# Two overlapping load slots in place of three separate ones, in a max-pooling kernel that streams its input

## The chip, the cores and the metric

The kernel runs on one core of a Trainium2 chip. The metric is the device time of one execution in microseconds (us).

A **window** here is one pooling window: 16 floats, 64 B, of which the maximum is kept. A load of n windows moves n x 64 B into each of the 128 partitions, that is n x 8192 B in all.

DVE is the vector engine, which does the poolings; SP and ACT are the engines that issue DMAs here. A DMA is spread over the core's 16 DMA engines: by the packet records each of them moves 8 of its 128 rows, one packet per row, and then signals a completion semaphore, a counter on which other engines wait. Where the text says that engines end apart, these 16 are meant.

## The reference, cut to what matters

```python
def setup_inputs():
    batch, channels, length = 32, 256, 4096
    output_size = 256
    return {"x": np.random.randn(batch, channels, length).astype(np.float32), ...}

def reference(x, output_size):
    for i in range(output_size):
        start = int(i * length / output_size)          # windows of 16
        end = int((i + 1) * length / output_size)
        result[:, :, i] = np.max(x[:, :, start:end], axis=-1)
    return result
```

134.22 MB are read, 8.39 MB are written, and nothing is read twice. Each partition handles 16384 windows.

## The kernel before

All the on-chip memory that the kernel uses is one area. At its low end are three load slots; from its high end the results grow downwards. As the results grow, the slots must shrink, so loads go from 1024 windows to 736.

```python
    SLOTS = 3
    MOST = 65536 // (4 * W)           # 1024 windows: 64 KB per partition
    FIRST = 128
    ...                               # sizes: 128, 1024 x2, 1000 x3, 940 x3, 884 x3,
    ...                               #        832 x3, 784 x3, 736, 152
    for g, loads in enumerate(groups):
        ...
        for i, size in enumerate(loads):
            a = b - size
            at = n_loads % SLOTS * slot_sizes[n_loads // SLOTS] * W
            slot = area[:, at : at + size * W]
            nc.sync.dma_start(out=slot, in_=xg[:, a * W : b * W])
            nc.vector.reduce_max(
                out=area[:, base + a : base + b],
                in_=slot.rearrange("p (n w) -> p n w", w=W),
                axis=mybir.AxisListType.X,
            )
            n_loads += 1
            b = a
        ...
    for dst, src in stores[1:2] + stores[0:1] + stores[2:]:
        nc.sync.dma_start(out=dst, in_=src)
```

Loads and stores are all issued from one engine (SP) into one queue. A load into a slot waits until the pooling of what was there is done. With three slots, two more loads are in the queue meanwhile.

## Time and profile before

| | kernel before |
|---|---|
| device time | 335.2 us (3 runs, 335.18 to 335.23) |
| span of the profiled run | 333.4 us |
| DMA queue busy | 99.2% of the span |
| DVE busy | 276.0 us (83%) |
| DMAs | 20 loads and 4 stores |

Lines of the page of the kernel before: busy time by engine, DMA packets, the DMA queue (packets, MB, share of the 16 DMA engines' time), the issues of the 1000-window loads (size, median us from issue to landing):

```profile
DVE 276.0 (83%) x20; POOL 0.2 (0%) x4
...
DMA packets 3456, 142.61 MB, mean 428 GB/s; under 512 B 384, under 2 KB 512, under 8 KB 512
...
q1 hardware_dynamic: 3456, 142.61, 99.2%
...
area<-in_x_dram SPq DMA_DIRECT2D x3, 8000.0 KB, 39.9
```

The queue is never idle between 1.75 and 332.1 us. A load takes 39.9 us from issue to landing, though it flows for only 19, because it stands in line behind another one.

The timeline of the kernel before. Columns: start in us, duration, engine, line, operation, result and input shapes, and in brackets the idle time before it and what ended that:

```profile
5.60 2.29 DVE L82 TENSOR_REDUCE area<-area 128x128 f32<-128x2048 f32 x1 [5.60 <-DMA area<-in_x_dram]
24.95 17.22 DVE L82 TENSOR_REDUCE area<-area 128x1024 f32<-128x16384 f32 x1 [17.06 <-DMA area<-in_x_dram]
44.30 17.22 DVE L82 TENSOR_REDUCE area<-area 128x1024 f32<-128x16384 f32 x1 [2.13 <-DMA area<-in_x_dram]
63.20 16.82 DVE L82 TENSOR_REDUCE area<-area 128x1000 f32<-128x16000 f32 x1 [1.68 <-DMA area<-in_x_dram]
...
281.35 13.22 DVE L82 TENSOR_REDUCE area<-area 128x784 f32<-128x12544 f32 x1 [1.54 <-DMA area<-in_x_dram]
296.18 13.22 DVE L82 TENSOR_REDUCE area<-area 128x784 f32<-128x12544 f32 x1 [1.61 <-DMA area<-in_x_dram]
```

DVE waits before every pooling but the last, so each of these starts when its load lands. The distance between two starts is the time in which one load flows: 19.35 us for 1024 windows, 14.83 for 784, in both cases 0.0189 us per window, whatever the size. The time is therefore the bytes over a fixed rate, plus a start, an end and small costs per DMA.

### The profile page before, as it was taken

What the parts mean: (1) busy time and instruction counts of PE and PEld (TensorE: products, weight loads), DVE (VectorE), ACT (ScalarE), POOL (GpSimd) and SP (SyncE); (2) the same over time, 40 slices, a digit from 0 to 9 for tenths busy, and PEclk for the clock granted to TensorE, in tenths of its full rate; (3) what the DMA queues carried; (4) which work ended last, traced back from release to release, by engine and by line L of the source; (5) the groups of instructions that cost most, each with busy time, mean ns of one, the idle gap of its engine ahead of it and who ended that gap; (6) DMA issues with size and microseconds to landing.
All of it is one profiled execution on the core that took longest, in us unless ns stands there. A gap on an engine that the chain in (4) does not pass through costs nothing.

```text
span 333.4 us, 113 instructions
## 1 busy us (share of the span) xinstructions
DVE 276.0 (83%) x20; POOL 0.2 (0%) x4
## 2 busy tenths in 40 slices
DVE  2009979797988989797989797989898898989990
POOL 0000000000000000000000000000000000000000
DMA  9898989898989998999999999999999999999997
GB/s 377 377 503 377 503 369 491 369 491 369 491 369 462 462 462 346 462 462 441 434 434 434 434 434 415 409 409 505 415 409 433 433 433 433 433 416 452 391 432 333
DMA packets 3456, 142.61 MB, mean 428 GB/s; under 512 B 384, under 2 KB 512, under 8 KB 512
## 3 DMA queue, kind: packets, MB, share of 16 engines
q1 hardware_dynamic: 3456, 142.61, 99.2%
HBM read 134.22 MB, written 8.39 MB: 428 GB/s over the span
## 4 chain that ended last, share of the span: by engine, by line
DMA 64%; DVE 31%; DVEq 1%; another core or an unknown queue 0%; SPq 0%; issue 0%
DMA area<-in_x_dram 64%; DVE area L82 31%; DVEq L129 1%; SPq L81 0%; DVEq L82 0%
## 5 line engine op out<-in xcount | busy, mean ns | idle before, releaser
L82 DVE TENSOR_REDUCE area<-area 128x1000 f32<-128x16000 f32 (+8 forms) x20 | 276.0, 13806 | 49.2 <-DMA area<-in_x_dram 49.2
L115 POOL MEMSET const-bfloat16-1.0<- 128x1 bf16 x1 | 0.1, 102 | 0.0
L115 POOL MEMSET const-uint8-127<- 128x1 uint8 x1 | 0.1, 102 | 0.0
L115 POOL MEMSET const-float32-0.0<- 128x1 f32 x1 | 0.1, 99 | 0.2 <-issue 0.2
L115 POOL MEMSET const-float32-1.0<- 128x1 f32 x1 | 0.1, 99 | 0.0
## 6 DMA issues: line engine op xcount, KB each, us to landing
area<-in_x_dram SPq DMA_DIRECT2D x3, 8000.0 KB, 39.9
area<-in_x_dram SPq DMA_DIRECT2D x3, 7520.0 KB, 37.5
area<-in_x_dram SPq DMA_DIRECT2D x3, 7072.0 KB, 35.3
area<-in_x_dram SPq DMA_DIRECT2D x3, 6656.0 KB, 33.2
area<-in_x_dram SPq DMA_DIRECT2D x3, 6272.0 KB, 31.3
area<-in_x_dram SPq DMA_DIRECT2D x1, 5888.0 KB, 30.3
out_dram<-area SPq DMA_DIRECT2D x1, 3934.0 KB, 27.4
out_dram<-area SPq DMA_DIRECT2D x1, 2966.0 KB, 33.7
```

Source lines behind the costliest of these rows:

```text
L82: nc.vector.reduce_max(out=area[:, base + a : base + b], in_=slot.rearrange("p (n w) -> p n w", w=W), axis=mybir.AxisListType.X,)
L115: nc = _bacc.Bacc("TRN2", target_bir_lowering=False, num_devices=1)
L129: with _tile.TileContext(nc) as tc:
```

## The change: intent and diff

The intent is fewer and larger transfers: 17 loads in place of 20. Two slots of 64 KB are left, and each swings by a gap of 152 windows (9.5 KB): a load lies alternately at the low and at the high end of its place. The part that the next load into the same place will cover (868 windows of 1020) is pooled first; the next load waits for that part only, and the other 152 windows are pooled afterwards. The results get memory of their own, so the loads no longer shrink.

```diff
-    SLOTS = 3
-    MOST = 65536 // (4 * W)
...
+    CHUNK = 1020
+    GAP = 152
+    FIRST = 152
+    LOADS_A, LOADS_B = 9, 6
...
+    ring = pool.tile([P, 2 * (CHUNK + GAP) * W], fp32, tag="ring", name="ring")
+    kept = pool.tile([P, total - last], fp32, tag="kept", name="kept")
...
+            low = n_loads % 2 * (CHUNK + GAP)
+            moved = n_loads // 2 % 2
+            at = low + moved * GAP
+            nc.sync.dma_start(
+                out=ring[:, at * W : (at + n) * W], in_=xg[:, a * W : (a + n) * W]
             )
+            if n == CHUNK:
+                dst = kept[:, base + a : base + a + n]
+                cut = CHUNK - GAP if moved else GAP
+                parts = [(0, cut), (cut, n)]
+                for u, v in parts if moved else parts[::-1]:
+                    pooled(dst[:, u:v], at + u, v - u)
+            else:
+                end = (at + CHUNK) * W
+                last_kept = ring[:, end - n : end]
+                pooled(last_kept, at, n)
...
+    for dst, src in stores:               # 9180, 152, 6120, 932 columns
         nc.sync.dma_start(out=dst, in_=src)
```

The changed kernel has loads of 152, 15 x 1020 and 932 windows and four stores.

More of the change, by code (lines that the diff above doesn't have):

```diff
@@ L32 @@
     assert B * C * O % P == 0
-    AREA = 53200
-    SLOTS = 3
-    MOST = 65536 // (4 * W)
-    ALIGN = 4
-    FIRST = 128
-    ROUNDS_A = 3
-    LAST = 4
-    slot_sizes = [MOST]
-    rounds = [[FIRST] + [MOST] * (SLOTS - 1)]
-    left = total - sum(rounds[0])
-    while left:
-        room = AREA - (total - left)
-        n = min(room // (SLOTS * W + SLOTS) // ALIGN * ALIGN, MOST)
-        if left <= slot_sizes[-1]:
-            n = left
-        slot_sizes.append(n)
-        rounds.append([])
-        while left and len(rounds[-1]) < SLOTS:
-            n = min(n, left)
-            rounds[-1].append(n)
-            left -= n
@@ L57 @@
-    sizes = [n for r in rounds for n in r]
-    groups = [sizes[:1], sizes[1 : ROUNDS_A * SLOTS], sizes[ROUNDS_A * SLOTS :]]
+    CHUNK = 1020
+    GAP = 152
+    FIRST = 152
+    LOADS_A, LOADS_B = 9, 6
+    last = total - FIRST - (LOADS_A + LOADS_B) * CHUNK
+    assert 0 < last and last * (W + 1) <= CHUNK * W
     pool = ctx.enter_context(tc.tile_pool(name="pool", bufs=1))
-    area = pool.tile([P, AREA], fp32, tag="area", name="area")
+    ring = pool.tile([P, 2 * (CHUNK + GAP) * W], fp32, tag="ring", name="ring")
@@ L63, with pooled, group @@
+    kept = pool.tile([P, total - last], fp32, tag="kept", name="kept")
     xw = x.flatten_outer_dims().rearrange("r (o w) -> (r o) w", w=W)
     ow = out.flatten_outer_dims().rearrange("r o -> (r o)")
+    def pooled(dst, at, n):
+        nc.vector.reduce_max(
+            out=dst,
+            in_=ring[:, at * W : (at + n) * W].rearrange("p (n w) -> p n w", w=W),
+            axis=mybir.AxisListType.X,
+        )
+    taken = 0
+    def group(n):
+        nonlocal taken
+        span = slice(taken * P, (taken + n) * P)
+        taken += n
+        return (
+            xw[span].rearrange("(p n) w -> p (n w)", p=P),
+            ow[span].rearrange("(p n) -> p n", p=P),
+        )
@@ L66 @@
+    xg, first_og = group(FIRST)
+    first_kept = kept[:, 0:FIRST]
+    nc.sync.dma_start(out=ring[:, CHUNK * W : (CHUNK + FIRST) * W], in_=xg)
+    pooled(first_kept, CHUNK, FIRST)
     stores = []
     n_loads = 0
-    first = 0
-    low = AREA
-    for g, loads in enumerate(groups):
-        n = sum(loads)
-        xg = xw[first : first + P * n].rearrange("(p n) w -> p (n w)", p=P)
-        og = ow[first : first + P * n].rearrange("(p n) -> p n", p=P)
-        first += P * n
-        base = low - n
-        b = n
-        for i, size in enumerate(loads):
-            a = b - size
-            at = n_loads % SLOTS * slot_sizes[n_loads // SLOTS] * W
-            slot = area[:, at : at + size * W]
-            nc.sync.dma_start(out=slot, in_=xg[:, a * W : b * W])
-            nc.vector.reduce_max(
-                out=area[:, base + a : base + b],
-                in_=slot.rearrange("p (n w) -> p n w", w=W),
-                axis=mybir.AxisListType.X,
-            )
-            n_loads += 1
-            b = a
-        low = base
-        if g < len(groups) - 1:
-            stores.append((og, area[:, base : base + n]))
-        else:
-            end = sum(loads[len(loads) - LAST :])
-            for a, b in ((end, n), (0, end)):
-                stores.append((og[:, a:b], area[:, base + a : base + b]))
@@ L97 @@
-    for dst, src in stores[1:2] + stores[0:1] + stores[2:]:
+    base = FIRST
+    for loads in ([CHUNK] * LOADS_A, [CHUNK] * LOADS_B + [last]):
+        xg, og = group(sum(loads))
+        a = 0
+        for n in loads:
+            low = n_loads % 2 * (CHUNK + GAP)
[3 more added lines that the diff above has]
+                out=ring[:, at * W : (at + n) * W], in_=xg[:, a * W : (a + n) * W]
+            )
+            if n == CHUNK:
[8 more added lines that the diff above has]
+                pooled(last_kept, at, n)
+            n_loads += 1
+            a += n
+        full = LOADS_A * CHUNK if len(stores) == 0 else LOADS_B * CHUNK
+        stores.append((og[:, 0:full], kept[:, base : base + full]))
+        base += full
@@ L98 @@
+    stores.insert(1, (first_og, first_kept))
+    stores.append((og[:, full : full + last], last_kept))
+    assert taken == total
+    for dst, src in stores:
         nc.sync.dma_start(out=dst, in_=src)
```

## The prediction

> **What bounds the kernel now.** The DMA queue. The page: 142.61 MB at a mean of 428 GB/s, the one hardware queue busy 99.2% of the 333.4 us span; DVE busy 276.0 us (83%), and its idle 49.2 us (the waits) all wait for loads. In the timeline, loads land at a constant rate: poolings of 1024 windows start 19.35 us apart (24.95 to 44.30), of 784 windows 14.76 to 14.83 us: 0.0189 us per window of 8192 B, 433 GB/s. The Trainium skill ("DMA: Bandwidth & Descriptors", "Where 436 GB/s comes from") puts the fabric ceiling at 435 GB/s; this trace agrees to 0.5%. The bytes don't change, so time can fall only by what is not bytes: start, end, per-packet costs.
>
> **What the change removes.** Three loads (20 to 17). The packet records show one packet per partition per DMA, 8 per engine: 65536 B took 2419 ns, 47104 B 1744 ns. A line through these has 0.03662 ns/B and leaves 19 ns per packet; a store's 31472 B took 1170 ns, as the line gives. So a DMA costs each engine 8 x 19 ns plus a 9 ns semaphore packet, 0.16 us. Three fewer: **-0.5 us** (an estimate from these). All of it is on the critical path: the queue never idles from 1.75 to 332.1 us.
>
> **What it adds.** (a) 13 more poolings. From 1000 windows 16.82 us and 736 windows 12.42 us, a pooling is 16.67 ns per window plus 0.15 us: +2 us of DVE, off the path. (b) Two slots for three: a load must now be issued while its predecessor flows. A load of 1020 windows flows 19.26 us. Last byte to start of pooling is 0.45 us; the first part, 868 windows, 14.62; semaphore and sequencer 0.1; issue to first packet 1.0 (first load: 0.73 to 1.75). Sum 16.2 us, and engines end a load up to 0.7 us apart: some 2.3 us of slack. Whole-slot poolings (17.2 us) would leave nearly none. So I expect no bubble. DVE needs 17.4 us per load, 1.8 under the period. (c) The end: the last load's 932 windows pool in 15.7 us; behind it flow stores of 9180, 152 and 6120 columns, 18.5 us by the line above; the last store could start 17.3 us after the last load's last byte, in time by 1.2 us. Before ends alike.
>
> **Predicted.** 335.2 - 0.5 = **334.7 us**, 8 in 10 between 334.3 and 335.7. Faster by over 2%: 0.01; within 2%: 0.96; slower by over 2%: 0.03.
>
> **What would show each step.** Right: DMA packets 3456 to 3024, the same 142.61 MB; the queue still above 99% of the span; 1020-window loads landing 19.2 to 19.3 us apart; DVE about 278 us; a load's time to landing (DMA issues) down from 39.9 to 22 to 23 us, as it is issued some 3 us before its predecessor ends. Wrong: a dip in the DMA row at each hand-over, landings over 19.5 us apart, or a hole of over 0.3 us before the last store.
>
> **What would make it wrong.** Issue to first packet much longer than the first load's 1.0 us: beyond 2.3 us more, each of 14 loads pays. Engines drifting over 2 us apart, so that early ones run dry, which two loads queued ahead hid before. A loss of 0.5 us per load would give 341.7 us, nearly the "slower" case. Some tenths of a us more or less at start or end move it within the range.

## More of the kernel before

One more line will matter, about the end of the program: SP's semaphore waits there, with first and last start:

```profile
L129 SPq EVENT_SEMAPHORE  x6: 17/28/28, 325.6 to 333.3; - x6
```

## The result, and the profile after

The changed kernel takes 335.32 us (median of 6 runs, 335.2 to 335.61), the kernel before in the same rounds 335.19 us (6 runs, 335.16 to 335.23). The ratio is 1.0005 with a 95% interval of 0.9993 to 1.0018: the same. (A ratio here is the mean time of one kernel's fast runs over that of the other's of the same rounds, so it isn't quite the ratio of the quoted medians. All runs are fast but one, of 349.89 us, of the kernel below that swings by 40 windows; the ratios leave it out.) The time lies in the stated range; the forecast gain of 0.5 us is not there.

Lines of the page of the changed kernel that answer to those above:

```profile
DVE 276.6 (83%) x32; POOL 0.2 (0%) x4
...
DMA packets 3025, 142.61 MB, mean 427 GB/s; under 512 B 337, under 2 KB 465, under 8 KB 593
...
q1 hardware_dynamic: 3024, 142.61, 99.0%
...
ring<-in_x_dram SPq DMA_DIRECT2D x15, 8160.0 KB, 23.9
```

Packets and bytes are as predicted. A load now takes 23.9 us from issue to landing (predicted: 22 to 23): it is issued while its predecessor flows, not two loads ahead.

The timeline of the changed kernel (two poolings of one load are merged into one line):

```profile
6.19 2.69 DVE L52 TENSOR_REDUCE kept<-ring 128x152 f32<-128x2432 f32 x1 [6.19 <-DMA ring<-in_x_dram]
25.53 17.21 DVE L52 TENSOR_REDUCE kept<-ring 128x868 f32<-128x13888 f32 x2 [16.65 <-DMA ring<-in_x_dram]
44.80 17.21 DVE L52 TENSOR_REDUCE kept<-ring 128x868 f32<-128x13888 f32 x2 [2.06 <-DMA ring<-in_x_dram]
...
295.38 17.21 DVE L52 TENSOR_REDUCE kept<-ring 128x868 f32<-128x13888 f32 x2 [2.07 <-DMA ring<-in_x_dram]
313.25 15.69 DVE L52 TENSOR_REDUCE ring<-ring 128x932 f32<-128x14912 f32 x1 [0.66 <-DMA ring<-in_x_dram]
328.97 0.33 SPq L110 DMA_DIRECT2D out_dram<-ring  x1
```

From 25.53 to 295.38 there are 14 loads: 19.275 us each, or 0.0189 us per window. That is the rate of before, so there is no hole at the hand-overs. The last load took 17.87 us; 932 windows at 0.0189 are 17.61.

The end of the changed kernel, SP's semaphore waits:

```profile
L141 SPq EVENT_SEMAPHORE  x6: 17/28/28, 332.8 to 333.8; - x6
```

In the kernel before, the first of these six waits was at 325.6 us, long before the end. Here the first is at 332.8 us, when the last store has landed, and the other five come after it. This turned out to be a cost.

### Where the tenths are

To see tenths of a microsecond I took a ruler to the packet records of the traces: the end of the last packet of a stage, less the bytes moved so far at 435.2 GB/s. (The ruler is the fabric ceiling that the Trainium skill gives in "DMA: Bandwidth & Descriptors", section "Where 436 GB/s comes from"; for comparing the sums any constant near it would do, as both kernels move the same bytes. The cost per DMA that is read from one row does depend on it: with 434.8 GB/s the second row would be about 0.27 us lower in each column.) All 142.61 MB take 327.7 us by it; the rest, in us, is in this table. The columns "again" are second traces of unaltered kernels, and "lanes" is an experiment below.

| what is not bytes | before | before, again | changed | changed, again | lanes |
|---|---|---|---|---|---|
| until the first load's last packet | 2.77 | 2.70 | 2.96 | 2.80 | 2.69 |
| loads up to the last but one (18, 18, 15, 15, 15 DMAs) | 1.24 | 1.29 | 1.08 | 1.03 | 1.05 |
| last load | 0.08 | 0.07 | 0.37 | 0.19 | 0.09 |
| stores (4, 4, 4, 4, 7 DMAs) | 0.30 | 0.32 | 0.21 | 0.24 | 0.37 |
| last packet to end of span | 1.31 | 1.29 | 1.53 | 1.54 | 1.31 |
| sum | 5.70 | 5.67 | 6.15 | 5.80 | 5.51 |

The sums differ by what the spans differ by (333.4, 333.3, 333.8, 333.5, 333.2 us). The trace in the column "changed" is of a run of 335.61 us, the slowest of the six; "changed, again" is of a run of 335.25 us. Three things can be read. By this ruler a DMA costs about 0.07 us in both kernels (1.24 / 18, 1.05 / 15), so three fewer save 0.2 us and not 0.5; an experiment below measures the cost without the ruler. The end is 0.23 us longer in the changed kernel, in both its traces. And its last load costs 0.1 to 0.3 us too much.

### The profile page after: what moved, and what is told of

The parts are those of the page before. It is cut to its first block, busy times and chain, and to the rows that moved or that the text cites. A ratio compares the mean times of both kernels' runs of the same rounds, so it can differ in the third digit from the quotient of the medians.

```text
span 333.8 us, 113 instructions
## 1 busy us (share of the span) xinstructions
DVE 276.6 (83%) x32; POOL 0.2 (0%) x4
## 2 busy tenths in 40 slices
DMA packets 3025, 142.61 MB, mean 427 GB/s; under 512 B 337, under 2 KB 465, under 8 KB 593
## 3 DMA queue, kind: packets, MB, share of 16 engines
q1 hardware_dynamic: 3024, 142.61, 99.0%
## 4 chain that ended last, share of the span: by engine, by line
DMA 63%; DVE 35%; SPq 0%; issue 0%; DVEq 0%
DMA ring<-in_x_dram 63%; DVE kept L52 31%; DVE ring L52 5%; SPq L87 0%; SPq L73 0%; DVEq L52 0%
## 5 line engine op out<-in xcount | busy, mean ns | idle before, releaser
L52 DVE TENSOR_REDUCE kept<-ring 128x152 f32<-128x2432 f32 (+1 forms) x31 | 260.9, 8456 | 51.7 <-DMA ring<-in_x_dram 51.7
L52 DVE TENSOR_REDUCE ring<-ring 128x932 f32<-128x14912 f32 x1 | 15.7, 15685 | 0.7 <-DMA ring<-in_x_dram 0.7
## 6 DMA issues: line engine op xcount, KB each, us to landing
ring<-in_x_dram SPq DMA_DIRECT2D x15, 8160.0 KB, 23.9
```

Of the source, the lines that this page charges most:

```text
L52: nc.vector.reduce_max(out=dst, in_=ring[:, at * W : (at + n) * W].rearrange("p (n w) -> p n w", w=W), axis=mybir.AxisListType.X,)
```

## The experiments

Twelve runs followed, two of them of the unaltered kernels. The theories at the start were: **A**, a DMA costs 0.16 us as predicted, and the gain was given back elsewhere; **B**, the fixed part of a packet overlaps the next packet, so a DMA costs nothing. A second question was the slack of the hand-over, which the prediction had put at 2.3 us.

### The changed kernel again, and the kernel before again

No edit.

> The changed kernel unaltered, to see what of its lost half microsecond repeats. Theory A (packet costs are real, -0.5 us, and the change gives the gain back at the start and in the last load): the median is 0.0 to 0.3 us over before, and the trace again has a first load that lands 0.1 to 0.2 us later than its bytes explain, and slow packets of over 2400 ns in the last load. Theory B (a packet's fixed 19 ns overlaps the next packet and costs no time): the same median, but the slow packets may be gone or elsewhere, and the landings stay 19.27 us apart. If the late landing is chance, this run falls on 335.2 us.

> The kernel before, unaltered, for a second trace: how much of the start (first load landing at 5.60 us), of the last load and of the end (1.31 us from last packet to end of span) repeats. Expected: the end within 0.02 us, as the order of the final waits is fixed in the program; the first load within 0.2 us; no slow packets in the last load; 335.2 us.

Measured: changed 335.34 us (5 runs, 335.21 to 335.6; ratio 1.0005, 0.9991 to 1.0018), before 335.15 us (4 runs). The traces are in the table. The end repeats (1.53 and 1.54 us against 1.31 and 1.29), so it belongs to the program. The late start does not: 2.96, then 2.80, against 2.77 and 2.70. The last load's slow packets do repeat: packets that take 2201 ns elsewhere took up to 2879 ns in the first trace and up to 2498 in the second. In neither trace of the kernel before is there such a packet in the last load.

### What a DMA costs

The kernel before, with each of its loads but the first cut in four DMAs. 57 DMAs are added, and slots and poolings are unchanged.

```diff
-            nc.sync.dma_start(out=slot, in_=xg[:, a * W : b * W])
+            k = 4 if size > FIRST else 1
+            cuts = [size * j // (k * ALIGN) * ALIGN for j in range(k)] + [size]
+            for u, v in zip(cuts, cuts[1:]):
+                nc.sync.dma_start(
+                    out=slot[:, u * W : v * W], in_=xg[:, (a + u) * W : (a + v) * W]
+                )
```

> The kernel before with every load but the first issued as four DMAs of a quarter each: 57 more DMAs, the same bytes, slots and poolings. Theory A (0.16 us of every engine per DMA): +9.1 us, 344 us, and 1000-window loads landing 19.4 us apart in place of 18.9. Theory B (the fixed part of a packet is hidden under its neighbour): within 0.5 us of before, landings still 18.9 us apart, and the sum of the packets' times exceeding the span of the queue.

Measured: 339.91 us against 335.22 (ratio 1.014, 1.0126 to 1.0154). Timeline of this kernel:

```profile
63.95 16.82 DVE L87 TENSOR_REDUCE area<-area 128x1000 f32<-128x16000 f32 x1 [2.00 <-DMA area<-in_x_dram]
83.03 16.82 DVE L87 TENSOR_REDUCE area<-area 128x1000 f32<-128x16000 f32 x1 [2.26 <-DMA area<-in_x_dram]
102.20 16.82 DVE L87 TENSOR_REDUCE area<-area 128x1000 f32<-128x16000 f32 x1 [2.35 <-DMA area<-in_x_dram]
```

The starts are 19.08 and 19.17 us apart, where they were 18.97 and 18.83 before (an average of 19.13 against 18.90). Both theories fall: 4.69 us for 57 DMAs are 0.082 us each, half of A's 0.16 and not B's nothing. The packet records give a reason for half: the 3 x 8 packets that an engine gains per load lengthen the sum of the packets' times by 13 ns each (a packet of 64000 B took 2363 ns, packets of 16128 and 15872 B took 605 and 596), not by the 19 ns that the prediction found by drawing a line through packets of 47 to 65 KB; and part of it overlaps: in this trace the times in which more than 16 packets are open at once (there are 16 engines) add up to 2.0 us per engine (0.6 in the kernel before). So three fewer DMAs are worth about 0.25 us.

### Which final wait comes last

The compiled programs show why the ends differ. The loads and stores use eight completion semaphores in turn, and at the end SP waits for all eight in a fixed order, two per instruction:

```
final waits on SP, in order:   (4, 3)   (5, 2)   (6, 1)   (7, 0)
before: 24 DMAs; the last store signals semaphore 7 -> waited for in the fourth instruction
changed: 21 DMAs; the last store signals semaphore 4 -> waited for in the first
```

In the trace, three satisfied waits follow that first one, which start 0.064 to 0.069 us apart. To test it, the smallest store (152 columns) was cut by partitions into four DMAs. That adds no packets, and shifts the last store to semaphore 7.

```diff
     for dst, src in stores:
-        nc.sync.dma_start(out=dst, in_=src)
+        rows = P // 4 if src is first_kept else P
+        for p in range(0, P, rows):
+            nc.sync.dma_start(out=dst[p : p + rows, :], in_=src[p : p + rows, :])
```

> The changed kernel with its store of 152 columns issued as four DMAs of 32 partitions each: the same packets, three DMAs more, so that the last store signals the semaphore that the program's end waits for last and not first. Theory C (in the changed kernel four final waits of 0.068 us stand in a row, the first for the last store, so three satisfied ones run after it): last packet to end of span falls from 1.535 us to about 1.33 us, median 0.1 to 0.2 us below the changed kernel. Rival (the longer end is the receipt of a store with short rows): the end stays 1.5 us and the median unchanged or 0.1 us worse.

Measured: 335.16 us (5 runs, 334.97 to 335.32), the kernel before in the same rounds 335.21; ratio 0.9999 (0.9986 to 1.0012). SP's waits at the end of this kernel:

```profile
L143 SPq EVENT_SEMAPHORE  x6: 17/28/28, 328.9 to 333.1; - x6
```

The first wait is back at 328.9 us, and from the last packet to the end of the span it is 1.31 us, not 1.53. The cause is shown: three more DMAs made the end 0.22 us shorter. The rival, the short rows of the last store, falls, because that store is unaltered. The median is 0.17 us below the changed kernel's, as the trace wants; the times alone don't separate it from the kernel before.

### The last load

Two tries at its 0.1 to 0.3 us. First, the last load cut in two DMAs of 780 and 152 windows, as the kernel before ends:

```diff
-            nc.sync.dma_start(
-                out=ring[:, at * W : (at + n) * W], in_=xg[:, a * W : (a + n) * W]
-            )
+            cuts = [0, n] if n == CHUNK else [0, n - FIRST, n]
+            for u, v in zip(cuts, cuts[1:]):
+                nc.sync.dma_start(
+                    out=ring[:, (at + u) * W : (at + v) * W],
+                    in_=xg[:, (a + u) * W : (a + v) * W],
+                )
```

> The changed kernel with its last load of 932 windows issued as two DMAs, of 780 and 152 windows, still pooled at once. If large packets at the turn from loads to stores cost the 0.26 us that the last load of the changed kernel took over its bytes, this gives it back: median about 0.2 us below the changed kernel. If those slow packets were chance or come from elsewhere: no difference beyond 0.1 us.

Measured: 335.22 us (335.16 to 335.57), ratio 1.0002 (0.999 to 1.0015). It has one DMA more, so its last store is waited for in the second instruction, and its end is 1.47 us in place of 1.54: that explains 0.07 us of the 0.12 us gained. The two pieces of the last load cost 0.07 and 0.21 us; small packets that should take 370 ns took up to 627. So the slowness is still there.

Second, the loads taken from the end of the rows to the start, as the kernel before does:

```diff
-        a = 0
+        a = sum(loads)
+        skip = sum(loads) - len([n for n in loads if n == CHUNK]) * CHUNK
         for n in loads:
+            a -= n
...                       # results and stores shifted to match
```

> The changed kernel with the loads of each group taken from the end of the rows to the start, as the kernel before does; sizes, slots and waits as they are. If the last load's lost 0.1 to 0.3 us has to do with where in memory it reads, it goes: the last packets take 2201 ns each, median 0.1 to 0.3 us below the changed kernel. If it comes from the turn to the stores or from engines ending apart, the slow last packets stay and the median too.

Measured: 335.29 us (335.26 to 335.53), ratio 1.0003 (0.9991 to 1.0015), and the last load cost 0.21 us by the ruler. So where it reads is not the reason. In the trace of the "lanes" kernel the last load cost only 0.09 us. There the engines had come out of the second load closer together (0.2 us apart, against 0.8 and 0.6 in the two traces of the changed kernel), and they stayed so to the end. Whether that is the cause was not tested: why the last load is slow stays open. In the first trace of the changed kernel ten of the eleven packets of over 2215 ns are the last ones of their engines (they start from 309.5 us on), and they still flow when the first store begins, at 311.97 us.

### How much slack the gap buys

First, no gap: each load waits for the whole of its slot.

```diff
-            moved = n_loads // 2 % 2
+            moved = 0
...
-                parts = [(0, cut), (cut, n)]
+                parts = [(0, n)]
```

> The changed kernel without the swing: each load waits until the whole of its slot is pooled (17.15 us in place of 14.6). Prediction's sum (issue to first packet 1.0 us): a load may start 18.7 us after its predecessor but one landed, against 19.28 us less 0.7 us of spread between engines: +0 to +2 us in all. If issue to first packet is longer with a nearly empty queue (2 us), a hole of 0.7 us or more per load, +10 us, 345 us. If it is far shorter, no loss at all and the gap was never needed.

Measured: 351.76 us (4 runs, 351.24 to 353.15), ratio 1.05 (1.048 to 1.052). Timeline:

```profile
44.54 17.15 DVE L52 TENSOR_REDUCE kept<-ring 128x1020 f32<-128x16320 f32 x1 [2.12 <-DMA ring<-in_x_dram]
65.90 17.15 DVE L52 TENSOR_REDUCE kept<-ring 128x1020 f32<-128x16320 f32 x1 [4.21 <-DMA ring<-in_x_dram]
85.81 17.15 DVE L52 TENSOR_REDUCE kept<-ring 128x1020 f32<-128x16320 f32 x1 [2.75 <-DMA ring<-in_x_dram]
```

Loads land 21.36 and 19.91 us apart, not 19.27, and on average 20.25. The gap is worth 16.4 us, where the prediction saw "nearly no" slack without it. The packet records show two costs of a late issue. An engine's first packet starts about 1.0 us after the issue, as in the first load (0.73 to 1.75 us); that had been counted. But these first packets then take up to 3.7 us in place of 2.4; that had not. It could have been seen in the first load of the kernel before as well: from issue to landing it took 4.8 us, of which the bytes explain 2.4.

From this I put a restart at 2.0 us and tried two smaller gaps:

```diff
+    STEP = 40          # the other kernel: 76
...
-            at = low + moved * GAP
+            at = low + moved * STEP
...
-                cut = CHUNK - GAP if moved else GAP
+                cut = CHUNK - STEP if moved else STEP
```

> The changed kernel swinging by 40 windows in place of 152: a load waits for 980 windows, 16.49 us, in place of 14.62. If a restart costs 2.0 us from issue (1.0 to the first packet and 1.0 more for slow first packets, as the whole-slot run suggests), some 0.3 us is lost per load: +4 us, about 339.5 us, and landings about 19.55 us apart. With the prediction's 1.0 us there is still 0.4 us to spare and no loss: 335.3 us.

> The changed kernel swinging by 76 windows: a load waits for 944 windows, 15.89 us. Both readings of the restart leave something to spare (0.3 us with 2.0 us, 1.3 us with 1.0 us), so both expect 335.3 to 335.6 us and landings 19.27 to 19.3 us apart. A loss here would say that a restart takes longer than 2.3 us or that engines drift apart by more than 0.7 us.

Measured: 343.81 us for 40 windows (342.2 to 349.89, with the slow run; the four fast runs alone have a median of 343.15; ratio 1.0242, 1.0222 to 1.0261) and 342.7 us for 76 (341.91 to 344.97; ratio 1.0237, 1.021 to 1.0264). That is a miss of both readings: 76 windows should have been free. I then guessed that an engine must know its next packet one packet ahead (theory D), in which case halved packets would need less lead:

```diff
-            nc.sync.dma_start(                       # in the kernel that swings by 76
-                out=ring[:, at * W : (at + n) * W], in_=xg[:, a * W : (a + n) * W]
-            )
+            cuts = [0, n // 8 * 4, n]
+            for u, v in zip(cuts, cuts[1:]):
+                nc.sync.dma_start(
+                    out=ring[:, (at + u) * W : (at + v) * W],
+                    in_=xg[:, (a + u) * W : (a + v) * W],
+                )
```

> The kernel that swings by 76 windows, with every load but the first issued as two DMAs of 32 KB rows: the first half is issued at the same moment after its predecessor landed (15.9 us), 2.7 us before the queue runs dry. Theory D (an engine must know its next packet about one packet ahead, so the lead that a seamless hand-over needs is the packet's 2.4 us plus some tenths): with packets of 1.2 us the 2.7 us suffice, the loss of 7.5 us vanishes and only 16 more DMAs of 0.07 to 0.08 us stay: 336.3 to 336.8 us, loads landing 19.3 to 19.4 us apart. Rival (a fixed lead of about 3 us, whatever the packet): the loss stays, 343 us or more.

Measured: 345.51 us (345.2 to 347.21), ratio 1.0317 (1.0292 to 1.0343). Theory D falls: the loss stays, and 16 more DMAs come on top. (The compiler's scheduler also moved some of the small poolings ahead of the large one, into DVE's idle time; the large one still starts when the load has landed.) The GB/s row of this kernel's page, in 40 slices, shows the dips at late hand-overs:

```profile
GB/s 327 429 435 439 431 417 431 429 426 407 421 431 432 431 421 426 388 421 435 432 431 368 445 426 425 393 409 427 421 430 377 433 427 413 435 415 428 430 408 261
```

The values of 388, 368, 393 and 377 are such dips; with 64 KB packets this row is too coarse to read. Last, a gap between:

```diff
+    STEP = 112
```

> The changed kernel swinging by 112 windows: a load waits for 908 windows, 15.29 us, so its issue leads the end of its predecessor by about 2.85 us, between the 3.5 us of 152 windows (no loss) and the 2.2 to 2.7 us of 76 (7.5 us lost). Theory D with one packet of 2.4 us and some tenths: no loss or little, 335.3 to 337 us. If the lead must be 3 us and more: several us lost, 338 to 342 us.

Measured: 336.95 us (336.86 to 337.34), ratio 1.0054 (1.0039 to 1.0069): 1.6 us over the changed kernel. Timeline of this one:

```profile
44.62 17.21 DVE L53 TENSOR_REDUCE kept<-ring 128x908 f32<-128x14528 f32 x2 [2.06 <-DMA ring<-in_x_dram]
63.96 17.21 DVE L53 TENSOR_REDUCE kept<-ring 128x908 f32<-128x14528 f32 x2 [2.13 <-DMA ring<-in_x_dram]
83.64 17.21 DVE L53 TENSOR_REDUCE kept<-ring 128x908 f32<-128x14528 f32 x2 [2.47 <-DMA ring<-in_x_dram]
102.96 17.21 DVE L53 TENSOR_REDUCE kept<-ring 128x908 f32<-128x14528 f32 x2 [2.11 <-DMA ring<-in_x_dram]
```

The first hand-over shown is nearly free (63.96 - 44.62 = 19.34), the next costs 0.4 us (19.68), the third is nearly free again (19.32). All of these together, with the **lead** worked out from the packet records: the time from the issue of the fourth load (152, 1020, 1020, then this one; the first that waits for a pooling) to the moment when the first engine has done its part of the load before. The losses are those of whole runs, not of that one hand-over.

| swing (windows) | lead at the first hand-over | median | loss against 335.33 |
|---|---|---|---|
| 152 (changed) | 3.5 and 3.7 us in two traces; later hand-overs down to 3.35 | 335.32, 335.34 | none |
| 112 | 3.0 us | 336.95 | 1.6 us |
| 76 | 2.7 us | 342.7 | 7.4 us |
| 76, halved packets | 2.1 us | 345.51 | 10.2 us (about 1.3 of it 16 more DMAs) |
| 40 | 1.9 us | 343.15 (fast runs) | 7.8 us |
| none | 1.4 us | 351.76 | 16.4 us |

So no load issued with a lead of 3.35 us or more lost time at its hand-over in the changed kernel, and in the kernels whose leads begin at 3.0 us or less there are losses. With 2.98 us (fifth load of the 112-window kernel) the first packets took 2680 ns on average and up to 3048, where with 3.48 us all took 2408. But a short lead does not lose every time. In the 40-window trace the fourth and the fifth load are both issued with 1.91 us:

```profile
44.59 17.21 DVE L53 TENSOR_REDUCE kept<-ring 128x980 f32<-128x15680 f32 x2 [2.06 <-DMA ring<-in_x_dram]
63.86 17.21 DVE L53 TENSOR_REDUCE kept<-ring 128x980 f32<-128x15680 f32 x2 [2.06 <-DMA ring<-in_x_dram]
85.33 17.21 DVE L53 TENSOR_REDUCE kept<-ring 128x980 f32<-128x15680 f32 x2 [4.25 <-DMA ring<-in_x_dram]
```

The fourth lands 19.27 us after the third, without loss; the fifth lands 21.47 us after the fourth, 2.2 us late. Nearly all of that kernel's loss comes from four such hand-overs (2.2, 1.9, 1.9 and about 1.3 us, the last at the last load). The last store of the changed kernel had a lead of only 1.3 us, and its first packet started with no gap; its rows are short (3728 B). So the lead tells from where on loads of this size are safe, not what one hand-over will cost.

In the 112-window kernel the loss also seems to feed itself. The next load is issued when the *slowest* engine's part has landed and been pooled, but the queue runs dry at the *fastest* engine, so whatever drives the engines apart eats the lead: in the 112-window kernel the engines' ends were 0.7 us apart at the fourth load and 1.4 us at the fifteenth, and the lead fell from 3.0 to between 2.2 and 2.6 us. In the 40-window kernel, though, the ends go from 0.5 us apart to 2.4 and back to 0.7 within three loads. Why a safe lead is three times the 1.0 us from issue to first packet, and why some hand-overs with less are free, was not found.

### A store beside the loads

A try for a version that beats both: the first group's store (4.7 MB) from ACT's queue in mid-run.

```diff
+        if len(stores) == 0:
+            nc.scalar.dma_start(out=og[:, 0:full], in_=kept[:, base : base + full])
+            stores.append(None)
+        else:
             stores.append((og[:, 0:full], kept[:, base : base + full]))
...
-    for dst, src in stores:
+    for dst, src in stores[1:]:
```

> The changed kernel with the store of its first group (4.7 MB) issued from ACT's queue as soon as it is pooled, in mid-run beside loads, not behind the last load. If a store's bytes take an engine's time as a load's do, nothing is gained: 335 to 337 us, loads landing up to 11 us later in total and the end that much shorter. If reads and writes of HBM can flow at once beyond 435 GB/s: up to 10.8 us less, 325 us.

Measured: 346.38 us (345.58 to 346.55), ratio 1.0328 (1.0313 to 1.0343): worse than either expectation. Timeline:

```profile
196.79 0.37 ACTq L104 DMA_DIRECT2D out_dram<-kept  x1
198.82 17.21 DVE L52 TENSOR_REDUCE kept<-ring 128x868 f32<-128x13888 f32 x2 [2.07 <-DMA ring<-in_x_dram]
230.68 17.21 DVE L52 TENSOR_REDUCE kept<-ring 128x868 f32<-128x13888 f32 x2 [14.64 <-DMA ring<-in_x_dram]
...
325.45 15.69 DVE L52 TENSOR_REDUCE ring<-ring 128x932 f32<-128x14912 f32 x1 [0.49 <-DMA ring<-in_x_dram]
341.17 0.33 SPq L114 DMA_DIRECT2D out_dram<-ring  x1
```

Beside the store one load took 31.86 us, 12.6 us longer than the others, for 4.7 MB that take 10.8 us at 435 GB/s. Nothing flows on top: the Trainium skill ("DMA: Bandwidth & Descriptors", "Issuing engines are not separate DMA queues") says that transfers from all issuing engines run on the same 16 DMA engines, and this run agrees. What the expectation missed is the end. The last pooling takes 15.7 us, and the stores behind the last load are what the queue does meanwhile. With 4.7 MB of them gone, the other two stores are done at 333.3 us, and the queue stands still until the first packet of the last store at 342.0 us (it is issued at 341.17 us, when the last pooling is done, 15.7 us after the last load landed). The late stores are therefore cover for the last pooling, not waste.

## Why the prediction was right or wrong, point by point

- **What bounds the kernel: right.** The queue stayed at 99% and loads land at 0.0189 us per window in both kernels. Only what is not bytes could change, and the time did not change by more than 0.1 to 0.2 us.
- **"So a DMA costs each engine 8 x 19 ns plus a 9 ns semaphore packet, 0.16 us": mis-sized.** It measures 0.08 us by the 57 added DMAs and 0.07 us by the table (with the ruler's constant as it is). The 19 ns came from extrapolating a line from packets of 47 to 65 KB down to zero, and from taking overlapping records as if they followed each other. The landing intervals of the kernel before could not have told: 0.16 us per DMA would make 784 windows dearer than 1024 by only 0.00005 us per window, or 0.04 us per load, and two intervals of 784 windows differ by 0.07 us (14.76 and 14.83). Three fewer DMAs give about -0.2 us, not -0.5.
- **"Before ends alike": wrong.** The last store comes in time, as predicted (its first packet started at 330.28 us, when the first engine became free), but issued only 1.3 us ahead of that, so, less the 1.0 us from issue to first packet, with about 0.3 us to spare and not 1.2. But the number of DMAs decides which of four final waits the last store is in; with 21 in place of 24 it is the first, which costs 0.22 us. This cancels the saving. The two are shown; the rest of the measured +0.1 us is in the last load (0.1 to 0.3 us, cause open) and in a start that varies by itself.
- **"13 more poolings [...]: +2 us of DVE": mis-sized, off the path.** They are 12 (32 against 20), and DVE's busy time went up by 0.6 us: two poolings of one load take 17.21 us together, one of 1020 windows 17.15 us, so a further pooling costs 0.06 us and not 0.15.
- **"Some 2.3 us of slack", "I expect no bubble": the second right, the first wrong.** There is no bubble at 152 windows, and landings are 19.27 us apart. But 112 windows, only 0.67 us later by the prediction's own sum, already lose 1.6 us. So the slack was not 2.3 us but under 0.67: the lead of 3.5 us is at most about half a microsecond over what is needed. The step that failed is "issue to first packet 1.0": the term is right as named, but loads were free of loss in every hand-over only with 3.35 us and more from issue. That 152 windows were enough is therefore in part luck, and so is a time within the stated range: the same sum would have promised no loss at 112 or 76 windows, which took 336.95 and 342.7 us. The time to landing was off for a related reason (23.9 us, not 22 to 23): the issue led by 3.5 us to the first engine's end and 4.3 us to the last one's, not by "some 3 us". The worry, issues too late and engines apart, names the right danger; it lay nearer than stated.
- **"Whole-slot poolings would leave nearly none": wrong in size.** They lose 16.4 us.

## What to carry to other kernels

When a queue is full and the bytes are fixed, count what is left before tuning it: here 5.7 us of 333, of which each DMA less could save only 0.07 to 0.08 us. Check a per-packet cost by cutting the transfers in pieces and timing that, as packet records overlap. And if a transfer is to be issued just in time, measure the lead by moving the issue until the time rises, with the spread of the DMA engines in it; a sum with the latency of the first load, on an empty queue, was about 2 us too small here for a hand-over that never loses.

## What the Trainium skill lacked or had wrong

- "DMA: Bandwidth & Descriptors" (section "Anatomy of one DMA — SWDGE (gpsimd) path") gives a fixed cost of about 2.0 us per DMA, for DMAs issued from GpSimd. It does not say what a DMA costs in a queue that is kept full: here 0.07 to 0.08 us (57 more DMAs: +4.69 us).
- The same page ("Latency and other measured facts") gives about 600 ns to the first byte for this queue. The first load agrees if counted from the end of the issue instruction (1.11 to 1.75 us). It does not say how long ahead of an emptying queue a transfer has to be issued: here, with 64 KB rows, loads with 3.35 us and more lost nothing, and kernels whose leads began at 3.0 us or less lost time in some of their hand-overs; halving the rows at a short lead did not help.
- No page that I read says how far the engines' finishing times lie apart, or that the distance can grow when transfers are issued late: 0.7 to 1.4 us over 11 loads with a gap of 112 windows, up to 2.5 us with 40.
- No page that I read tells of the final waits for the completion semaphores, or that their fixed order costs 0.064 to 0.069 us for each that stands behind the last store's: 1.53 against 1.31 us from last packet to end.
